# Conditioning products of a two-block transformer: four of six groups summed per partition on VectorE, then one matmul per slice

## The chip, the cores and the metric

The kernel runs on one core of one Trainium2 chip. The metric is the device time of one execution in microseconds, the median of several. In the rows PE is TensorE's matmul, PEld its weight load, DVE is VectorE, ACT is ScalarE, POOL is GpSimd, SP is SyncE, whose queue issues all DMAs here.

## What is computed

Two transformer blocks follow one another on 256 tokens of 1024 features, all in float32. The first has two layers (a stick-breaking and a dilated attention, each with a feed-forward part `ffn1` of width 4096 and a gated per-layer input). The second has two layers (a latent attention with pooling, a grouped attention, each with a convolutional feed-forward part `ffn2`) and a second stream of 256 context tokens. The second block is conditioned: for each of its layers two vectors, the one of the batch (`c`) and the one of the context (`c_ctx`), are multiplied with a matrix of 1024 x 6144. This is the part that the change is about:

```python
    for i in range(DEPTH):
        ...
        ml = (jax.nn.silu(c) @ w_mod[i] + b_mod[i]).reshape(B, N_MOD, 1, D)
        mc = (jax.nn.silu(c_ctx) @ w_mod[i] + b_mod[i]).reshape(N_MOD, D)
        hl = modulate(xl, ml[:, 0], ml[:, 1])
        hc = modulate(xc, mc[0], mc[1])
```

The six rows of 1024 (shift, scale and gate, twice) are taken in three groups of 2048 columns. Of the last layer's second and third group only the row of `c` is used, since the context stream ends there.

## The kernel before

Weights come in tiles of 128 x 1024 float32 through four buffers `ws`; ScalarE rounds each tile to a high part `wh`, VectorE subtracts it to get the low part `wl` (lines 182 and 183, in halves of 512 columns, four buffers each), and TensorE multiplies the three products of high and low parts (lines 194 to 196). The program is written in one order, with generators as fillers: while the main stream goes on, `fill` takes steps from queues, `ctx` (the context stream, which works in the PSUM banks `fx`), `mod` (the conditioning products) and `main`. The numbers of the table `FILL` say how many units of filler go in at each place. Tile's scheduler then sets the order of each engine.

`gemv_gen` computes a group of conditioning rows: for each of eight blocks of 128 input features it loads two `ws` tiles and multiplies them on TensorE, with the two conditioning columns (padded to 32) as weights and four column strips of the array, in one bank `fx` that stays taken until the group is done (line 465). VectorE adds the bias and the one (line 469). Groups 0 and 1 of the first conditioned layer are done in the stick-breaking mixer; group 2 in the first `ffn1`; the second layer's group 0, 1 and 2 in the dilated mixer (where `attend` is the attention of a pair of heads and `proj` projects the next) and in the second `ffn1`. In `ffn1` each of 16 steps is an `up` of the next 256 hidden features, a filler, and a `down` of the last ones.

## Time and profile before

| | |
|---|---|
| median of 3 runs | 1740.43 us (1735.95 to 1746.13) |
| span of the profiled execution | 1732.4 us |
| busy: TensorE / its weight loads | 1662.8 / 1428.1 us |
| busy: VectorE / ScalarE / GpSimd | 1106.5 / 925.7 / 42.3 us |
| DMA | 337.72 MB, 195 GB/s on the mean |
| conditioning matmuls (L465) | 384 records, 65.0 us busy, 35 to 823 us from the start |

The span is that of one execution that the profiler took, from its first to its last instruction; its own device time is not listed, and the span lies 8.0 us below the median of the runs and 3.5 below the lowest. The stretches used below are 190 to 460 us (the first layer's end of mixer, `ffn1` and gate), 460 to 690 (the dilated mixer) and 690 to 900 (the second `ffn1`). Busy times of an engine are a union of its records; matmuls overlap each other in the pipeline, so that the distance between starts says more than the duration of one.

### The profile page before, as it was taken

What the parts mean: (1) busy time and instruction counts of PE and PEld (TensorE: products, weight loads), DVE (VectorE), ACT (ScalarE), POOL (GpSimd) and SP (SyncE); (2) the same over time, 40 slices, a digit from 0 to 9 for tenths busy, and PEclk for the clock granted to TensorE, in tenths of its full rate; (3) what the DMA queues carried; (4) which work ended last, traced back from release to release, by engine and by line L of the source; (5) the groups of instructions that cost most, each with busy time, mean ns of one, the idle gap of its engine ahead of it and who ended that gap; (6) DMA issues with size and microseconds to landing.
All of it is one profiled execution on the core that took longest, in us unless ns stands there. A gap on an engine that the chain in (4) does not pass through costs nothing.

```text
span 1732.4 us, 28608 instructions
## 1 busy us (share of the span) xinstructions
PE 1662.8 (96%) x10465; PEld 1428.1 (82%) x10468; DVE 1106.5 (64%) x2153; ACT 925.7 (53%) x1853; POOL 42.3 (2%) x65
## 2 busy tenths in 40 slices
PE   7998999999999999999999999999999999989997
PEld 6767888987887667888888988988999987779997
DVE  4437644557775446744667777767666887766665
ACT  5536544556654435544556556755555555545554
POOL 0000000000000000000000000000000000000000
PEclk9999999999999999999999999999999999989999
DMA  7777577654666666676756655446666765246663
GB/s 237 259 260 250 178 243 260 215 182 142 212 193 211 206 193 206 198 255 231 226 173 191 201 164 166 131 146 202 188 204 188 244 197 169 67 153 186 186 187 99
DMA packets 301073, 337.72 MB, mean 195 GB/s; under 512 B 18400, under 2 KB 246180, under 8 KB 300932
## 3 DMA queue, kind: packets, MB, share of 16 engines
q1 hardware_dynamic: 300932, 335.89, 61.7%
q8 instruction: 82, 1.34, 0.3%
q14 instruction: 59, 0.48, 0.1%
HBM read 332.57 MB, written 3.24 MB: 194 GB/s over the span
## 4 chain that ended last, share of the span: by engine, by line
PE 45%; DMA 5%; DVE 5%; ACT 2%; issue 1%; POOL 1%; SPq 0%; POOLq 0%; ACTq 0%; DVEq 0%
PE mm L196 6%; PE mm L194 6%; PE mm L195 6%; PE acc L195 5%; PE acc L196 5%; PE acc L194 5%; PE fx L196 3%; PE fx L194 3%; PE fx L195 3%; DMA ws<-in_w_ff_out 2%; DMA ws<-in_w_ff_in 2%; DVE wl L183 2%; PE acc L1007 1%; ACT wh L182 1%; PE mm L1033 1%
## 5 line engine op out<-in xcount | busy, mean ns | idle before, releaser
L183 DVE TENSOR_TENSOR wl<-ws,wh 128x512 fp32r<-128x512 f32 x1004 | 638.9, 668 | 402.7 <-ACT wh L182 391.4
L182 ACT CAST wh<-ws 128x512 fp32r<-128x512 f32 x1004 | 567.4, 603 | 510.3 <-PE mm L195 125.2
L194 PE MATMUL mm<-uh,wh 128*128 128x256 f32 x1344 | 382.8, 285 | 2.9 <-ACT wh L182 2.2
L196 PE MATMUL mm<-uh,wl 128*128 128x256 f32 x1344 | 382.0, 284 | 0.9 <-DVE wl L183 0.9
L195 PE MATMUL mm<-ul,wh 128*128 128x256 f32 x1344 | 381.6, 284 | 0.0
L194 PEld LDWEIGHTS mm<-uh,wh 128*128 128x128 f32 x1344 | 258.7, 192 | 8.7 <-ACT wh L182 3.0
L195 PEld LDWEIGHTS mm<-ul,wh 128*128 128x128 f32 x1344 | 258.8, 193 | 3.0 <-issue 0.4
L196 PEld LDWEIGHTS mm<-uh,wl 128*128 128x128 f32 x1344 | 258.7, 192 | 2.1 <-DVE wl L183 1.9
L194 PE MATMUL acc<-wh,hh 128*128 128x512 f32 x432 | 172.1, 398 | 0.0
L196 PE MATMUL acc<-wh,hl 128*128 128x512 f32 x432 | 169.6, 393 | 0.0
L195 PE MATMUL acc<-wl,hh 128*128 128x512 f32 x432 | 169.2, 392 | 0.0
L194 PEld LDWEIGHTS acc<-wh,hh 128*128 128x128 f32 x432 | 81.3, 188 | 28.7 <-ACT wh L182 5.9
L196 PE MATMUL fx<-uch,wl 128*128 128x256 f32 x352 | 100.6, 286 | 2.9 <-DVE wl L183 2.8
L194 PE MATMUL fx<-uch,wh 128*128 128x256 f32 x352 | 101.0, 287 | 1.7 <-DVE fsum L1191 1.7
L195 PE MATMUL fx<-ucl,wh 128*128 128x256 f32 x352 | 100.4, 285 | 0.0
L196 PEld LDWEIGHTS acc<-wh,hl 128*128 128x128 f32 x432 | 81.2, 188 | 18.3 <-issue 0.8
L195 PEld LDWEIGHTS acc<-wl,hh 128*128 128x128 f32 x432 | 81.4, 188 | 14.8 <-issue 0.4
L194 PE MATMUL mm<-wh,uh 128*128 128x384 f32 (+1 forms) x256 | 86.0, 337 | 2.1 <-ACT wh L182 1.6
L195 PE MATMUL mm<-wl,uh 128*128 128x384 f32 (+1 forms) x256 | 83.3, 325 | 0.6 <-DVE wl L183 0.6
L196 PE MATMUL mm<-wh,ul 128*128 128x384 f32 (+1 forms) x256 | 82.9, 324 | 0.0
L216 POOL TENSOR_TENSOR s<-s,neghalf 128x1 f32<-128x1 f32 (+2 forms) x52 | 38.7, 744 | 1556.5 <-DVE s L214 1556.5
L465 PE MATMUL fx<-ws,cst 128*32 128x512 f32 x384 | 65.0, 607 | 6.7 <-DMA ws<-in_w_mod 5.7
(397 smaller groups left out, 2658.9 us busy)
## 6 DMA issues: line engine op xcount, KB each, us to landing
ws<-in_ffn_w_up SPq DMA_DIRECT2D x528, 128.0 KB
ws<-in_w_mod SPq DMA_DIRECT2D x96, 512.0 KB
ws<-in_ffn_w_down SPq DMA_DIRECT2D x66, 512.0 KB
ws<-in_w_ff_in SPq DMA_DIRECT2D x64, 512.0 KB
ws<-in_w_ff_out SPq DMA_DIRECT2D x64, 512.0 KB
ws<-in_w_in_dil SPq DMA_DIRECT2D x96, 192.0 KB
ws<-in_w_in_sb SPq DMA_DIRECT2D x24, 512.0 KB
row<-mod SPq DMA_DIRECT2D x19, 512.0 KB
```

Source lines behind the costliest of these rows:

```text
L182: act.copy(out=h[:, s], in_=st[:, s])
L183: vec.tensor_sub(out=l[:, s], in0=st[:, s], in1=f32(h[:, s]))
L194: pe.matmul(o, lh, rh, start=start, stop=False)
L195: pe.matmul(o, lh, rl, start=False, stop=False)
L196: pe.matmul(o, ll, rh, start=False, stop=stop)
L216: gp.tensor_tensor(out=r, in0=v, in1=neghalf.to_broadcast([128, w]), op=ALU.pow)
L465: pe.matmul(ps[32 * q:32 * q + 32, :], cst[:, kc, :], st[:, q2 * 512:(q2 + 1) * 512], start=kc == 0, stop=kc == 7)
L1007: pe.matmul(sc[qt][:, n * 256:(n + 1) * 256], q(hd, qt), k(hd, n), start=True, stop=True)
L1033: pe.matmul(o, v(hd, n, kt), PTs[hd][:, 2 * n + kt, :], start=n == 0 and kt == 0, stop=n == nk - 1 and kt == 1)
```

## The change

Four of the six groups leave TensorE's loop. `gemv_vec` loads the same `ws` tiles, but VectorE multiplies a tile with a conditioning value per partition and adds it into an accumulator `ga` of 128 x 1024, over the eight blocks; then four matmuls with `sel` (zero but for its first column, which is one) sum a slice over the partitions. For the groups of which only the row of `c` is used (`nr` = 1) one slice covers all 2048 columns and each tile is read once for one row; with both rows (`nr` = 2) a group has two slices of 1024 columns, and each tile is used for two rows. Group 2 of the first conditioned layer goes into the first `ffn1` (one tile per step), group 0 of the second into the dilated mixer (one tile per `yield` of `attend`), its groups 1 and 2 into the second `ffn1` (two tiles per step). The `mod` queue is empty after the first mixer; so in the last round of the dilated attention `ctx_ok` is true and the context stream fills it. The context fill of the first `ffn1` has 1.6 units in each of 13 steps where it had 5.04 in the four steps after the conditioning group.

```diff
-FILL = dict(sb1=5.0, sb2=1.25, sb3=0.5, sb_end=6.0, sbd=6.0, sbm=0.8, m0=1.0, mix0=8.5, mix1=8.5, f1c=5.04,
+FILL = dict(sb1=5.0, sb2=1.25, sb3=0.5, sb_end=6.0, sbd=6.0, sbm=0.8, m0=1.0, mix0=8.5, mix1=8.5, f1c=1.6,
...
+    sel = const.tile([128, 32], F32, name="sel")
...
+    gp.memset(sel, 0.0)
+    gp.memset(sel[:, 0:1], 1.0)
...
+    def gemv_vec(p, tag, bufs, i, grp, nr):
...
+        w = a["w_mod_2"][i]
+        for half in range(nr):
+            c0 = grp * 2048 + half * 1024
+            accs = [p.tile([128, 2, 512], F32, tag=tag, name="ga", bufs=bufs) for _ in range(2)]
+            for kc in range(8):
+                for hf in range(3 - nr):
+                    st = stage()
+                    c1 = c0 + hf * 1024
+                    nc.sync.dma_start(out=st, in_=w[kc * 128:(kc + 1) * 128, c1:c1 + 1024])
+                    for r in range(nr):
+                        o = accs[hf + r].rearrange("p q n -> p (q n)")
+                        c = cst[:, kc, r:r + 1]
+                        if kc == 0:
+                            vec.tensor_scalar(out=o, in0=st, scalar1=c, scalar2=None, op0=ALU.mult)
+                        else:
+                            vec.scalar_tensor_tensor(out=o, in0=st, scalar=c, in1=o, op0=ALU.mult, op1=ALU.add)
+                    yield
+            clean("ctx")
+            one = one_t[:, grp:grp + 1] if nr == 1 else float(2 * grp + half in (1, 4))
+            bt = fillp.tile([128, 512], F32, tag="xd", name="gvb", bufs=2)
+            gp.memset(bt, 0.0)
+            ps = fx1()
+            mt = tmp((128, 512))
...
+            for q in range(4):
+                pe.matmul(ps[32 * q:32 * q + 32, :], sel, accs[q // 2][:, q % 2, :], start=True, stop=True)
+            vec.scalar_tensor_tensor(out=mt, in0=ps, scalar=one, in1=bt, op0=ALU.add, op1=ALU.add)
...
+            def gemvs():
+                for args in (((0, 2, 2),) if i == 0 else ((1, 1, 1), (1, 2, 1))):
+                    yield from gemv_vec(p, "ga", 2, *args)
+
+            gv = gemvs()
             up(0)
             for g in range(G):
                 if g + 1 < G:
                     up(g + 1)
-                if i == 1 or g_mod0b in queues["mod"]:
-                    fill(1, "mod")
+                next(gv, None)
+                if i == 1:
+                    pass
                 elif g < G - 3:
                     fill(FILL["f1c"])
                 elif g == G - 3:
                     until_dense(FILL["f1d"])
                 if g == G - 2:
+                    clean("ctx")
+                    for _ in gv:
+                        pass
                     before_end()
                 down(g)
+                if i == 1:
+                    next(gv, None)
...
+            gv = gemv_vec(fillp, "c4", 11, 1, 0, 2)
             for qr in range(4):
                 if qr < 3:
                     queues["main"].append(proj(qr + 1))
                 ctx_ok[0] = qr == 3 and not queues["mod"]
                 for t in attend(qr, fx1 if qr < 3 else mm1):
                     work(t)
-                    if qr < 3:
-                        fill(FILL["dlm"], "mod")
+                    next(gv, None)
                 drain_main()
+                if qr == 2:
+                    for _ in gv:
+                        pass
...
-    g_mod0a, g_mod0b, g_mod1 = gemv_gen(0, (0, 1)), gemv_gen(0, (2,)), gemv_gen(1, range(3))
-    queues["mod"].extend([g_mod0a, g_mod0b, g_mod1])
+    g_mod0a = gemv_gen(0, (0, 1))
+    queues["mod"].append(g_mod0a)
```

The scheduler decides where these instructions stand. SP's queue in the second `ffn1`, before (`in_w_ff_in` feeds an `up`, `in_w_ff_out` a `down`, `in_w_mod_2` the conditioning; all go into `ws`, and the numbers are those of single buffers):

```order
L176 DMA ws_7658<-in_w_ff_in 128x4x256
L176 DMA ws_7666<-in_w_ff_in 128x4x256
L462 DMA ws_7730<-in_w_mod_2 128x1024
L462 DMA ws_7734<-in_w_mod_2 128x1024
L176 DMA ws_7738<-in_w_ff_out 128x1024
L176 DMA ws_7758<-in_w_ff_out 128x1024
```

The same queue there after the change:

```order
L490 DMA ws_8129<-in_w_mod_2 128x1024
L177 DMA ws_8132<-in_w_ff_in 128x4x256
L177 DMA ws_8140<-in_w_ff_in 128x4x256
L490 DMA ws_8204<-in_w_mod_2 128x1024
L177 DMA ws_8207<-in_w_ff_out 128x1024
L177 DMA ws_8227<-in_w_ff_out 128x1024
L490 DMA ws_8247<-in_w_mod_2 128x1024
```

The two conditioning loads of a step now stand apart, one behind the `up` loads and one behind the `down` loads, in every step but the last ones.

VectorE in the second `ffn1`, before (`wl` is a half of a weight tile's low part, `r` and `hl` belong to the hidden features):

```order
L623 TENSOR_TENSOR r_7843<-r_7843 128x512
L183 TENSOR_TENSOR wl_7901<-ws_7898,wh_7900 128x512 x2
L200 TENSOR_TENSOR hl_7847<-r_7843,hh_7846 128x512
L183 TENSOR_TENSOR wl_7909<-ws_7906,wh_7908 128x512 x2
L183 TENSOR_TENSOR wl_7981<-ws_7978,wh_7980 128x512 x2
L183 TENSOR_TENSOR wl_8001<-ws_7998,wh_8000 128x512 x2
L623 TENSOR_TENSOR r_7963<-r_7963 128x512
```

And after the change, about the same step:

```order
L201 TENSOR_TENSOR hl_7965<-r_7961,hh_7964 128x512
L184 TENSOR_TENSOR wl_8092<-ws_8089,wh_8091 128x512 x2
L497 SCALAR_TENSOR_TENSOR ga_7613<-ws_8129,cst_102,ga_7613 128x1024
L184 TENSOR_TENSOR wl_8112<-ws_8109,wh_8111 128x512 x2
L497 SCALAR_TENSOR_TENSOR ga_7612<-ws_8204,cst_102,ga_7612 128x1024
L184 TENSOR_TENSOR wl_8135<-ws_8132,wh_8134 128x512 x2
L184 TENSOR_TENSOR wl_8143<-ws_8140,wh_8142 128x512
L665 TENSOR_TENSOR r_8079<-r_8079 128x512
```

The six halves between `hl` and the next `r` follow each other before; now a multiply-add `ga` stands behind the first pair and another behind the second, five and three rows ahead of the next `r`.

VectorE in the dilated mixer at the first softmax of the third pair of heads, before (`s` and `P` are the softmax's sums and probabilities, `acc` its scores):

```order
L683 TENSOR_REDUCE s_6363<-acc_6353 128x1
L685 TENSOR_SCALAR s_6365<-s_6363 128x1
L183 TENSOR_TENSOR wl_6482<-ws_6478,wh_6481 128x512
L183 TENSOR_TENSOR wl_6482<-ws_6478,wh_6481 128x256
L689 RECIPROCAL s_6369<-s_6367 128x1
L683 TENSOR_REDUCE s_6373<-acc_6353 128x1
L690 TENSOR_SCALAR P_6362<-P_6362,s_6369 128x384
```

And after the change at the same place:

```order
L736 TENSOR_REDUCE s_6348<-acc_6338 128x1
L497 SCALAR_TENSOR_TENSOR ga_6268<-ws_6564,cst_102,ga_6268 128x1024
L738 TENSOR_SCALAR s_6350<-s_6348 128x1
L497 SCALAR_TENSOR_TENSOR ga_6269<-ws_6564,cst_102,ga_6269 128x1024
L742 RECIPROCAL s_6354<-s_6352 128x1
L736 TENSOR_REDUCE s_6358<-acc_6338 128x1
L743 TENSOR_SCALAR P_6347<-P_6347,s_6354 128x384
```

Two multiply-adds now stand inside the softmax, between the maximum (L736) and the normalisation (L743), where a tile's two `wl` stood; both read the same `ws` tile.

## Rows read from the trace of the kernel before

**Rows 1.** The page, part 1: busy us of each engine, share of the span, instructions.

```profile
PE 1662.8 (96%) x10465; PEld 1428.1 (82%) x10468; DVE 1106.5 (64%) x2153; ACT 925.7 (53%) x1853; POOL 42.3 (2%) x65
```

**Rows 2.** The page, part 4: shares by engine of the chain that ended last.

```profile
PE 45%; DMA 5%; DVE 5%; ACT 2%; issue 1%; POOL 1%; SPq 0%; POOLq 0%; ACTq 0%; DVEq 0%
```

**Rows 3.** Timeline of TensorE, second `ffn1`, with a filler: start us, us, instruction.

```profile
746.24 1.07 PE L465 MATMUL fx<-ws,cst 128*32 128x512 f32 x8
...
747.23 0.50 PE L194 MATMUL acc<-wh,hh 128*128 128x512 f32 x1
...
759.66 0.50 PE L194 MATMUL acc<-wh,hh 128*128 128x512 f32 x1
```

**Rows 4.** The same timeline, later steps without a filler.

```profile
847.69 0.40 PE L194 MATMUL acc<-wh,hh 128*128 128x512 f32 x1
...
858.91 0.40 PE L194 MATMUL acc<-wh,hh 128*128 128x512 f32 x1
```

**Rows 5.** Stretches: busy us (records) of PE, PEld, DVE, ACT, POOL; clock, DMA share, GB/s.

```profile
460.00:690.00 230.00, 219.75 (x1258) 168.80 (x1261) 128.18 (x314) 110.63 (x251) 4.57 (x7) 0.99 0.65 201
690.00:900.00 210.00, 205.61 (x1333) 179.85 (x1332) 122.47 (x197) 104.30 (x190) 2.57 (x4) 1.00 0.67 219
610.00:620.00 10.00, 6.92 (x41) 5.44 (x38) 4.92 (x14) 4.22 (x12) 0.00 (x0) 0.91 0.73 225
620.00:630.00 10.00, 10.00 (x44) 6.63 (x43) 4.04 (x12) 3.83 (x10) 0.00 (x0) 0.75 0.26 79
760.00:780.00 20.00, 20.00 (x124) 17.11 (x123) 10.22 (x17) 8.44 (x15) 0.00 (x0) 1.00 0.84 283
```

**Rows 6.** The same view, line L465 (conditioning matmuls) alone.

```profile
190.00:460.00 270.00, 8.52 (x64) 1.26 (x64) 1.00 0.63 207
460.00:690.00 230.00, 26.22 (x128) 3.60 (x128) 0.99 0.65 201
690.00:900.00 210.00, 8.53 (x64) 1.26 (x64) 1.00 0.67 219
```

**Rows 7.** Waits of TensorE's weight loads, 460 to 690: us, times, longest.

```profile
PEld fx L465 <- DMA ws<-in_w_mod: 7.2, 6, 3.5
...
PEld fx L760 <- DVE wl L183: 1.2, 2, 0.8
...
PEld fx L760 <- DVE s L685: 0.8, 1, 0.8
```

**Rows 8.** Groups of VectorE by shape, whole span: busy us, mean ns, idle before.

```profile
L183 DVE TENSOR_TENSOR wl<-ws,wh 128x512 fp32r<-128x512 f32 x934 | 613.8, 687 | 397.0 <-ACT wh L182 385.7 <-issue 0.3
...
L481 DVE SCALAR_TENSOR_TENSOR h<-t,s,h 128x1024 f32<-128x1024 f32 x8 | 10.2, 1278 | 0.0
...
L690 DVE TENSOR_SCALAR P<-P,s 128x768 f32<-128x768 f32 x8 | 4.9, 613 | 0.0
...
L469 DVE SCALAR_TENSOR_TENSOR t<-fx,misc,gvb 128x512 f32<-128x512 f32 x6 | 4.5, 749 | 8.0 <-PE fx L465 8.0
```

**Rows 9.** Timelines of SP's queue, ScalarE and TensorE, second `ffn1`.

```profile
744.00 1.62 SPq L176 DMA_DIRECT2D ws<-in_w_ff_in  x2
...
747.33 0.81 SPq L462 DMA_DIRECT2D ws<-in_w_mod  x2
...
748.91 0.62 ACT L182 CAST wh<-ws 128x512 fp32r<-128x512 f32 x1 [4.50 <-DMA ws<-in_w_ff_in]
...
758.66 1.06 PE L465 MATMUL fx<-ws,cst 128*32 128x512 f32 x8
```

**Rows 10.** ScalarE's casts, 720 to 820: busy us, mean ns, idle before by releaser.

```profile
L182 ACT CAST wh<-ws 128x512 fp32r<-128x512 f32 x60 | 34.5, 618 | 53.8 <-DMA ws<-in_w_ff_in 27.2 <-DMA ws<-in_w_ff_out 25.9 <-PE mm L195 0.3
```

**Rows 11.** Timeline of TensorE, second layer's `ffn2`, steps without a filler.

```profile
1606.25 0.40 PE L194 MATMUL acc<-wh,hh 128*128 128x512 f32 x1
...
1614.75 0.40 PE L194 MATMUL acc<-wh,hh 128*128 128x512 f32 x1
```

**Rows 12.** Line L465, whole span: what TensorE idled for before it, us, times.

```profile
  DMA ws<-in_w_mod: 16.0, 16
```

More of the change, by code (lines that the diff above doesn't have):

```diff
@@ L474, in gemv_gen @@
             yield 0.1
+    def gemv_vec(p, tag, bufs, i, grp, nr):
[23 more added lines that the diff above has]
+            for q in range(4):
+                c1 = c0 + (q if nr == 1 else q % 2) * 512
+                nc.sync.dma_start(out=bt[32 * q:32 * q + 1, :], in_=a["b_mod_2"][i:i + 1, c1:c1 + 512])
+            for q in range(4):
+                pe.matmul(ps[32 * q:32 * q + 32, :], sel, accs[q // 2][:, q % 2, :], start=True, stop=True)
+            vec.scalar_tensor_tensor(out=mt, in0=ps, scalar=one, in1=bt, op0=ALU.add, op1=ALU.add)
+            for q in range(4):
+                c1 = c0 + (q if nr == 1 else q % 2) * 512
+                r = 0 if nr == 1 else q // 2
+                nc.sync.dma_start(out=mod[i][r:r + 1, c1:c1 + 512], in_=mt[32 * q:32 * q + 1, :])
+            yield
+        mod_done.add((i, grp))
     def post_norm(y, g, tt):
@@ L1108, in ffn2 @@
                     up(f + 1)
-                if i == 0 and g_mod1 in queues["mod"]:
-                    fill(1, "mod")
-                elif i == 0 and f < NCH - 3:
+                if i == 0 and f < NCH - 3:
                     credit["ctx"] += FILL["f2c"]
```

## The prediction

> **What bounds the kernel now.** I read the busy times first: TensorE is busy for 96% of the span, VectorE 64%, ScalarE 53% [rows 1], and the chain that ended last is mostly TensorE's [rows 2]. A busy matmul engine may still be one that waits inside its pipeline, so the next view is the distance between starts. In the second layer's `ffn1` one loop step (an `up`, a filler, a `down`) takes 759.66 - 747.23 = 12.43 us while the filler is a conditioning step [rows 3], and 858.91 - 847.69 = 11.22 us once there is no filler [rows 4]. Steps that repeat like this while VectorE is busy only 122 of that stretch's 210 us [rows 5] are steps of a full TensorE. So a conditioning step (8 matmul records) costs 12.43 - 11.22 = 1.21 us of the end time there, somewhat more than the 1.07 us that its records show [rows 3].
>
> Where the removed work sits comes from its line cut into stretches: 64 records in the first layer's `ffn1` (190 to 460), 128 in the dilated mixer (460 to 690), 64 in the second `ffn1` (690 to 900) [rows 6]. That is 8, 16 and 8 steps; the other 128 of 384 lie earlier and stay. The dilated mixer is less clean: 128 records there are busy 26.22 us, 1.64 us a step, and TensorE's weight loads wait 7.2 us for these very transfers [rows 6, 7].
>
> **The change part by part.**
>
> *Removed.* 32 steps of 1.21 us: -9.68 us in each `ffn1`, -19.36 us in the mixer.
>
> *Added on TensorE.* Six slices end with four matmuls (8 records) of the form of the old ones, so 1.21 us each, two in each stretch: +2.42 us three times. That leaves -7.26, -16.94 and -7.26 us, together -31.5 us.
>
> By the busy rows alone it would be -43.27 + 43.27 x 48/256 = -35.2 us [rows 6]. The Trainium skill ("Trainium Kernel Development and Optimization", Performance Expectations) calls matmul busy time a bad metric because matmuls are pipelined. By that rule the sum from starts, -31.5 us, is the one to keep; the trace agrees, since 1.64 us of busy per step in the mixer stands against 1.21 us between starts.
>
> *Added on VectorE.* 84 multiply-adds of 128x1024 with two tensors and a column: the same operation and shape takes 1278 ns at L481 [rows 8], 107 us together. 12 products of 128x1024 with a column: nearest row 613 ns for 768 elements [rows 8], scaled 0.82 us, 10 us. VectorE goes from 1106 to about 1223 us, 72% of the new span. Locally, a step of the second `ffn1` has ten operations of about 0.687 us (eight `wl`, `r`, `hl`) [rows 8] and now two of 1.28: 9.4 us in 11.22. It fits, and the cover is the 1.8 us left. Were that gone (VectorE at 11.5 us), each step would lose 0.3 us. A multiply-add would have to take (11.22 - 6.87)/2 = 2.2 us before VectorE became the limit; I take 1.28, since shape, operation and memory are those of the row.
>
> *The new wait.* At the end of a slice VectorE waits for the four matmuls, as it does today at L469 [rows 8]: 8.0 us over six, thus 1.3 us each, and this now happens eight times instead of six. Behind it stand the `wl` of the next weights. Two more such waits, 2.7 us, are below what the range holds; I take nothing.
>
> *Feed.* The second `ffn1` now has two conditioning loads in all but the last steps, as the filled steps have today, but a step shall last 11.22 us instead of 12.43: six loads of 524 KB, 280 GB/s instead of 253. It has run at 283 GB/s over 20 us in that very stretch [rows 5]. The four `ws` buffers must turn over in 4/6 of a step, 7.5 us. A weight load issued at 744.00 is taken up by ScalarE at 748.91, 4.9 us later [rows 9]; two casts and two subtractions and the issue bring that to about 7.3 us, a conditioning load to about 6.6. Today the conditioning loads sit longer: issued at 747.33, used by TensorE at 758.66, over 11 us [rows 9]. So it fits narrowly, and ScalarE already waits for loads much of the time [rows 10]. Bounds: 0, or the pace of today (12.43 us in all 16 steps, which is +17 us against the sum). I take +2 us, near the lower end, because of the 283 GB/s.
>
> *Mixer.* Here the removed steps were also cover for the softmax chain on VectorE and ScalarE, while multiply-adds now stand in that chain's queue. On the other side the 7.2 us of waits for the loads can vanish. Bounds: -7.2 us, or one 1.28 us multiply-add ahead of each of the 15 chain steps of three head pairs, +19.2 us, plus a fall of the clock like the one at 610 to 630, where TensorE was busy 6.92 of 10 us and the granted clock then stood at 0.91 and 0.75, part of the time at 1.2 instead of 2.4 GHz (0.9 + 2.5 = 3.4 us lost) [rows 5]: +22.6 us. Today that chain is late by under 1 us at a time [rows 7]. I take 0: the two cancel.
>
> *Moved.* The context fill of the first `ffn1` is spread as 13 x 1.6 = 20.8 units where it was 4 x 5.04 = 20.2: nothing. With `mod` empty, the last attention round of the mixer is filled with context work that came later before, down to the first `ffn2`. That stage stays full without it: in the second layer, with no filler, steps repeat at 1614.75 - 1606.25 = 8.50 us and so does the next [rows 11]. Nothing; if that cover failed, some of the 18.8 units that the round asks for (3.38 + 7.65 + 2 x 2.4 + 3.0, about a us each) would be missed later. 16 more short bias loads and stores (0.3 to 0.4 us each on SP as other issues [rows 9]) hide in SP's idle time; 6 us if not. The two extra memsets lie on GpSimd, idle all but 42 us [rows 1].
>
> **Sum:** -31.5 + 2.0 = -29.5 us. The profiled execution has a span of 1732.4 us, 8.0 below the median of the runs, 1740.43; keeping that distance, 1702.9 of span and **1711 us** measured (-1.7%). This case's own range is 1704 to 1719: the two extra waits, the feed between 0 and twice what I took, and a mixer that keeps or loses 5 us.
>
> **Rivals.**
>
> *More than the sum.* All 7.2 us of waits for the loads vanish and the feed costs nothing: -31.5 - 7.2 = -38.7, 1702 us. For it: conditioning loads no longer wait 11 us for TensorE's turn. Against: the chain in the mixer loses cover.
>
> *The loads pace the second `ffn1`.* 16 steps at 12.43 us are 198.9 us against 8 x 12.43 + 8 x 11.22 = 189.2 today: +9.7 there instead of -5.3, in all -14.5, 1726 us. For it: ScalarE's waits [rows 10]; against: 283 GB/s.
>
> *The mixer gives it back* (the change frees TensorE only for it to idle): -7.3 - 5.3 + 5.7 = -6.9, 1734 us, no measurable change. For it: the chain's rows from VectorE are there already [rows 7]; against: VectorE is busy 128 of 230 us there, and 39 us more still leave a quarter.
>
> *Slower, by VectorE's queue.* Each of the 64 loads is now awaited on VectorE, and the `wl` of the next weights stand behind. TensorE's waits for such loads were 16.0 us in 16 times [rows 12]; at 1.0 us for every load, all passed on, +64 - 31.5 = +32.5, 1773 us. It cancels the gain at 0.49 us a load and makes the kernel slower beyond the measurement's reach at 0.63. The Trainium skill ("TensorE: Matmul & The Clock Gate", Architectural detail) says that VectorE is strict FIFO; no run here shows it yet. By that rule nothing can pass a waiting multiply-add. Against the rival: the loads are issued in the order in which VectorE takes them, and there are four buffers.
>
> **Chances.** Forecast 0.50, more 0.15, loads pace 0.13, mixer gives back 0.14, slower 0.08. A difference under 0.5% (8.7 us) can hardly be told from none here. Forecast, more and loads pace lie beyond it on the fast side: faster 0.78. The mixer case and a little of its neighbours: same 0.14; slower 0.08. The range runs from a little under the second case to the mixer case, 1698 to 1735; it leaves out the slower case and the tail of the mixer's.
>
> **What would show it.** Right: steps of about 11.2 to 11.4 us in both `ffn1`, 48 matmul records at the new line, multiply-adds of about 1.28 us, VectorE near 1223 us, TensorE's busy time lower by about 35 us, no waits of TensorE for conditioning loads after 200 us. Wrong: steps of 12 us or more in the second `ffn1` with ScalarE or VectorE waiting for loads (feed), idle TensorE before L813 and L833's transposes in the mixer with a granted clock under 0.97 there (chain), or `wl` late behind a multiply-add that waits for its load (queue).

## The result and the profile after

The changed kernel takes 1723.22 us (median of 4 runs, 1721.61 to 1724.47) against 1742.59 for the kernel before (4 runs, 1735.95 to 1746.13): a ratio of 0.9892, 95% interval 0.9866 to 0.9919. It is faster, by 19.4 us or 1.1%, beyond the 0.5% that can be told from nothing. The forecast was 1711 us with 1704 to 1719 as its own range, so the sign and the wide range (1698 to 1735) held, and the size did not: the time lies 12 us above the forecast, and of the 29.5 us that were to be gained 10 are missing.

The traced execution has a span of 1720.3 us, 12.1 less than that of before. Since one run here took 1722.1 us with a span of 1720.3, the span of 1732.4 before belongs, by the same distance, to an execution of some 1734 us (an estimate), at the low end of its kernel's; the last 7 us of the difference between the medians lie in executions of which there is no trace.

First the page's line on engines, which answers to [rows 1]:

```profile
PE 1635.5 (95%) x10259; PEld 1428.7 (83%) x10260; DVE 1211.1 (70%) x2251; ACT 926.6 (54%) x1854; POOL 44.6 (3%) x69
```

TensorE's busy time fell by 27.3 us (about 35 were expected) and VectorE's rose by 104.6 (117 were expected). The prices of the new instructions were near, as the groups of VectorE by shape show (columns as in [rows 8]):

```profile
L497 DVE SCALAR_TENSOR_TENSOR ga<-ws,cst,ga 128x1024 f32<-128x1024 f32 x84 | 106.3, 1281 | 57.7 <-DMA ws<-in_w_mod 57.5
L495 DVE TENSOR_SCALAR ga<-ws,cst 128x1024 f32<-128x1024 f32 x12 | 8.7, 749 | 1.9 <-DMA ws<-in_w_mod 1.9
```

A multiply-add takes 1.281 us where 1.278 was taken, a product 0.749 where 0.82 was. What was not in the sum stands behind the second bar, the idle time ahead of these instructions: VectorE waited 57.5 + 1.9 us for these 64 loads, 0.93 us each.

Where the time went is read by stages. Each `ffn1` is counted from the first matmul of its first `up` to the start of the last `acc<-wh,hh` of its last `down`, read from TensorE's timeline; the mixer from the gate's products behind the first `ffn1` to the second `ffn1`. The borders of the mixer and of the second `ffn1`, before and then after:

```profile
452.13 0.39 PE L194 MATMUL acc<-wh,uh 128*128 128x512 f32 x1
...
705.72 0.39 PE L194 MATMUL mm<-uh,wh 128*128 128x256 f32 x1 [0.33 <-DVE ul L200]
...
903.44 0.39 PE L194 MATMUL acc<-wh,hh 128*128 128x512 f32 x1
```

```profile
452.60 0.39 PE L195 MATMUL acc<-wh,uh 128*128 128x512 f32 x1
...
696.99 0.39 PE L195 MATMUL mm<-uh,wh 128*128 128x256 f32 x1
...
903.53 0.39 PE L195 MATMUL acc<-wh,hh 128*128 128x512 f32 x1
```

| stage | before | after | change | forecast |
|---|---|---|---|---|
| up to the first `ffn1` | 203.3 | 205.3 | +2.0 | 0 |
| first `ffn1` | 228.9 | 227.7 | -1.2 | -7.3 |
| up to the gate's products | 19.9 | 19.6 | -0.3 | 0 |
| gate's products and dilated mixer | 253.6 | 244.4 | -9.2 | -16.9 |
| second `ffn1` | 197.7 | 206.5 | +8.8 | -5.3 |
| up to the next gate's products | 17.0 | 20.7 | +3.7 | 0 |
| latent attention and first `ffn2` | 487.8 | 470.2 | -17.6 | 0 |
| the rest | 324.2 | 325.9 | +1.7 | 0 |

The mixer, the gate behind the second `ffn1` and the first `ffn2` belong together: 17.8 us of context products (106 more matmul records, start to start) moved into the mixer's last round, 3.7 us (39 records) into that gate, and they are missing later. By subtraction the mixer without them became 27 us shorter. The busy times, clock and DMA of the mixer and the second `ffn1`, the first two stretches of [rows 5]:

```profile
460.00:690.00 230.00, 221.30 (x1332) 191.25 (x1332) 182.35 (x381) 127.73 (x285) 6.21 (x10) 0.99 0.63 188
690.00:900.00 210.00, 194.72 (x1199) 170.99 (x1198) 149.54 (x216) 93.82 (x170) 1.48 (x2) 0.98 0.77 249
```

In the mixer VectorE is busy 182 of 230 us. The granted clock is 0.99 as before, and the loads that TensorE waited for in [rows 7] are no longer among its waits. In the second `ffn1` TensorE is busy 10.9 us less, and the stage nevertheless takes longer. Its step, from TensorE's timeline as in [rows 3]:

```profile
758.87 0.40 PE L195 MATMUL acc<-wh,hh 128*128 128x512 f32 x1
...
772.35 0.40 PE L195 MATMUL acc<-wh,hh 128*128 128x512 f32 x1
...
785.85 0.40 PE L195 MATMUL acc<-wh,hh 128*128 128x512 f32 x1
```

13.48 and 13.50 us, where 11.22 was expected and 12.43 stood before. Not all steps are like these: of the 13 distances from the first `down` to the 14th, six are 11.22 to 11.47 us and seven 12.5 to 14.0 (two of these at the end of the first group). In the long ones TensorE waits for a low part that VectorE makes late (between 710 and 830 us; us in total, times, longest), which it did for 0.2 us before:

```profile
PE mm L197 <- DVE wl L184: 7.1, 5, 2.0
```

The timelines of SP's queue, ScalarE and VectorE in the step from 758.87 on say why:

```profile
757.07 0.38 SPq L177 DMA_DIRECT2D ws<-in_w_ff_in  x1
759.60 0.34 SPq L490 DMA_DIRECT2D ws<-in_w_mod  x1
...
761.73 0.62 ACT L183 CAST wh<-ws 128x512 fp32r<-128x512 f32 x1 [0.32 <-DMA ws<-in_w_ff_in]
762.26 0.59 ACT L664 ACTIVATE r<-mm 128x512 f32<-128x512 f32 x1
...
764.54 1.28 DVE L497 SCALAR_TENSOR_TENSOR ga<-ws,cst,ga 128x1024 f32<-128x1024 f32 x1 [3.77 <-DMA ws<-in_w_mod]
765.74 1.89 DVE L184 TENSOR_TENSOR wl<-ws,wh 128x512 fp32r<-128x512 f32 x3
767.55 0.69 DVE L665 TENSOR_TENSOR r<-r 128x512 f32<-128x512 f32 x1
768.15 0.68 DVE L184 TENSOR_TENSOR wl<-ws,wh 128x512 fp32r<-128x512 f32 x1
...
771.57 1.29 DVE L497 SCALAR_TENSOR_TENSOR ga<-ws,cst,ga 128x1024 f32<-128x1024 f32 x1 [0.76 <-DMA ws<-in_w_mod]
...
778.04 1.28 DVE L497 SCALAR_TENSOR_TENSOR ga<-ws,cst,ga 128x1024 f32<-128x1024 f32 x1 [3.98 <-DMA ws<-in_w_mod]
```

The conditioning load is issued at 759.60, and VectorE stands idle for 3.77 us until it can be read. Behind it stand the low parts of two tiles that ScalarE cast from 760.27 on, and the square of `r`, which ScalarE had made by 762.85. The second `up` tile was issued at 757.07 and is let go at 768.83: its buffer was held for 11.8 us, where the working said 7.3. SP then waits for buffers, and the next loads come late. The Trainium skill ("TensorE: Matmul & The Clock Gate", Architectural detail) calls VectorE's queue strict FIFO; the trace agrees here: `r` stood ready for 4.7 us, and in the first 1.7 of them the engine did nothing.

From the multiply-add at 764.54 to the one at 778.04 are 13.50 us: 8.7 of work on VectorE and 0.76 + 3.98 of waits for two loads, with nothing else between. So in this stretch the step is as long as VectorE's work and waits together. Later steps with the same work are 11.22 us because the waits are short. VectorE's waits for the loads over three long steps (745 to 786 us) and over three short ones (826 to 859):

```profile
DVE ga L497 <- DMA ws<-in_w_mod: 16.1, 7, 4.0
```

```profile
DVE ga L497 <- DMA ws<-in_w_mod: 3.0, 4, 1.0
```

Why the later loads come in time is not shown by any run.

### The profile page after: what moved, and what is told of

The parts are those of the page before. It is cut to its first block, busy times and chain, and to the rows that moved or that the text cites. A ratio compares the mean times of both kernels' runs of the same rounds, so it can differ in the third digit from the quotient of the medians.

```text
span 1720.3 us, 28310 instructions
## 1 busy us (share of the span) xinstructions
PE 1635.5 (95%) x10259; PEld 1428.7 (83%) x10260; DVE 1211.1 (70%) x2251; ACT 926.6 (54%) x1854; POOL 44.6 (3%) x69
## 4 chain that ended last, share of the span: by engine, by line
PE 55%; DVE 14%; DMA 13%; issue 4%; ACT 3%; SPq 1%; POOL 1%; ACTq 0%; POOLq 0%; DVEq 0%
PE mm L195 6%; PE mm L196 6%; PE mm L197 6%; PE acc L197 6%; PE acc L196 6%; PE acc L195 6%; DMA ws<-in_w_mod 6%; DVE wl L184 5%; PE fx L195 4%; PE fx L196 4%; PE fx L197 4%; DMA ws<-in_w_ff_in 2%; DVE ga L497 2%; DMA ws<-in_w_in_dil 2%; ACT wh L183 1%
## 5 line engine op out<-in xcount | busy, mean ns | idle before, releaser
L184 DVE TENSOR_TENSOR wl<-ws,wh 128x512 fp32r<-128x512 f32 (+1 forms) x1004 | 638.1, 668 | 273.3 <-ACT wh L183 261.5
L183 ACT CAST wh<-ws 128x512 fp32r<-128x512 f32 (+1 forms) x1004 | 568.6, 604 | 477.8 <-PE mm L196 132.7
L497 DVE SCALAR_TENSOR_TENSOR ga<-ws,cst,ga 128x1024 f32<-128x1024 f32 x84 | 106.3, 1281 | 57.7 <-DMA ws<-in_w_mod 57.5
L195 PEld LDWEIGHTS acc<-wh,hh 128*128 128x128 f32 x432 | 82.2, 190 | 17.6 <-issue 1.6
```

Source lines behind the costliest of these rows:

```text
L183: act.copy(out=h[:, s], in_=st[:, s])
L184: vec.tensor_sub(out=l[:, s], in0=st[:, s], in1=f32(h[:, s]))
L195: pe.matmul(o, lh, rh, start=start, stop=False)
L497: vec.scalar_tensor_tensor(out=o, in0=st, scalar=c, in1=o, op0=ALU.mult, op1=ALU.add)
```

## The experiments

**The second `ffn1`: whose fault is it?** Three edits, each alone in the changed kernel, and one that spreads the load. Each ratio is to the kernel before as measured beside the run; the changed kernel was not measured again, so differences to it of a few us whose ratios overlap its own (0.9866 to 0.9919) are no firmer than that. First, its two groups back on TensorE:

```diff
-            gv = gemvs()
+            gv = gemvs() if i == 0 else iter(())
+            g_ff = gemv_gen(1, (1, 2)) if i == 1 else None
+            if i == 1:
+                queues["mod"].append(g_ff)
...
                 if i == 1:
-                    pass
+                    fill(1, "mod")
```

> Only the two groups of the second ffn1 go back to TensorE's loop; the other two stay on VectorE. That stage takes 206.5 us after the change (697.0 to 903.5 in the trace) and took 197.7 before (705.7 to 903.4). Theory 1 (loads that are awaited on VectorE, and a burst of them at the end, cost more than the removed matmuls gave): the stage returns to about 198 us, the span falls by about 9 us to 1711, measured 1713 against 1723. Theory 2 (the 8.8 us are a shift between stages, work that was late anyway): the span stays at 1718 to 1722.

Measured 1737.39 us (7 runs, 1728.05 to 1743.34; ratio to before 0.9963, 0.9937 to 0.999), 14 us slower than the changed kernel. The stage took 212.8 us and the gate behind it 6 us more. Neither theory's number: my comparison with before was wrong, since before held 8 conditioning steps in this stage and this kernel 16 (the other 8 were in the mixer). With equal work, VectorE is much the cheaper place even with its waits.

Second, the loads left out:

```diff
-                    st = stage()
-                    c1 = c0 + hf * 1024
-                    nc.sync.dma_start(out=st, in_=w[kc * 128:(kc + 1) * 128, c1:c1 + 1024])
+                    if get:
+                        st = get()
+                    else:
+                        st = stage()
...
+            get = (lambda: h[:, 0, :]) if i == 1 else None
```

> In the second ffn1 the multiply-adds read a tile that lies in SBUF all the time (the residual), and the 32 conditioning loads are left out, so two conditioning rows are wrong. All VectorE work stays. Theory 1 (the wait for loads): steps of 11.2 to 11.5 us all through, the stage about 190 us (197.7 - 8 x 1.21 + 2.4), span about 1704. Rival (VectorE's own time for the multiply-adds is the cost): steps stay at 13 to 14 us while they run, stage over 203 us, span over 1717.

Measured 1710.30 us (one run), span 1708.5; the steps 11.22 us but for two at the end of the first group (13.97 and 12.42), the stage 185.8. With no load to stand behind, the scheduler put up to five multiply-adds into one step and none into others, and those with five are 11.22 us too. Full multiply-adds cost nothing when they wait for nothing: the rival (VectorE's own time) falls, in the form that its time by itself is the cost. Third, the loads kept and the multiply-adds made short:

```diff
-                        if kc == 0:
+                        if nr == 1 and kc:
+                            o = o[:, 0:16]
+                            vec.scalar_tensor_tensor(out=o, in0=st[:, 0:16], scalar=c, in1=o, op0=ALU.mult, op1=ALU.add)
+                        elif kc == 0:
```

> In the second ffn1 all conditioning loads stay and are awaited on VectorE at the same places, but 28 of 32 multiply-adds work on 16 columns of 1024 (their sums are wrong). Theory 1 (the wait at the head of VectorE's queue and the four buffers): most of the loss stays, steps of 12.3 to 13.5 us, the stage 200 to 206 us, span 1714 to 1720. Rival (VectorE's own time): steps of 11.2 us, the stage about 191, span 1705.

Measured 1712.69 us (one run), span 1710.9, the stage 196.3; steps of 11.22 us with all loads in place (11.69 to 13.97 around the end of the first group), though VectorE still waited for them between 720 and 830 us, longer than in the changed kernel (there first, then here):

```profile
DVE ga L497 <- DMA ws<-in_w_mod: 25.3, 12, 4.0
```

```profile
DVE ga L496 <- DMA ws<-in_w_mod: 29.9, 13, 4.7
```

My theory 1 falls too, in the form that the wait by itself is the cost. What remained was the end of the stage. The two runs bracket the cost: 8.7 us of VectorE's work and more fit into 11.22 us, and so do 6.6 of work with 4 to 5 of waiting; 8.7 with 4.7 do not, and the step grows to their sum. Why the loads are late is then a third theory, a loop. Each of six tiles holds one of four buffers from its issue until VectorE has read it; waits and operations on VectorE lengthen the holding, and late buffers make late loads.

The end of the stage has a cause of its own. In the changed kernel the generator is emptied at the last step but one. SP's queue, ScalarE, and the stretches of the stage's end there:

```profile
871.36 9.16 SPq L490 DMA_DIRECT2D ws<-in_w_mod  x5
```

```profile
886.89 1.14 ACT L183 CAST wh<-ws 128x512 fp32r<-128x512 f32 x2 [7.28 <-DMA ws<-in_w_ff_out]
```

```profile
880.00:892.00 12.00, 8.04 (x49) 5.66 (x48) 9.59 (x13) 4.45 (x9) 0.00 (x0) 0.88 0.87 295
892.00:904.00 12.00, 12.00 (x46) 9.65 (x46) 7.25 (x13) 5.78 (x12) 0.55 (x1) 0.83 0.63 191
```

Five conditioning loads pass ahead of the last weights, ScalarE waits 7.28 us for these, TensorE is busy 8.04 of 12 us, and the granted clock stands at 0.88 and then 0.83, part of the time at 1.2 instead of 2.4 GHz. From the 14th `down` on it takes 32.6 us to the stage's last `acc<-wh,hh`, against 22.1 before and 23.0 in the run without the loads. The 14th `down` before and then after:

```profile
881.35 0.40 PE L194 MATMUL acc<-wh,hh 128*128 128x512 f32 x1
```

```profile
870.93 0.40 PE L195 MATMUL acc<-wh,hh 128*128 128x512 f32 x1
```

The edit against it:

```diff
                 if i == 1:
                     next(gv, None)
+                    if g in (1, 3, 5, 7):
+                        next(gv, None)
```

> As the changed kernel, but in four of the early steps of the second ffn1 a third conditioning tile is taken, so that none is left over for the end, where now five loads in a row stand ahead of the last weights (the last two steps and the end take 32.6 us from the 14th down on, 22.1 before). Theory 1a (the burst by itself costs about 10 us, and an earlier tile costs about 2 us in its step, four of them): the stage falls by 2 to 10 us, span 1711 to 1718, and ScalarE's wait of 7.3 us before the last weights is gone. Rival (the loads cost the same wherever they stand): span 1720 to 1724.

Measured 1720.20 us (4 runs, 1717.23 to 1726.36; ratio to before 0.9856, 0.9831 to 0.988), 3 us under the changed kernel with overlapping runs. The stage took 203.9 us in the trace, which is of the slowest of the four runs: the end is shorter (28.1 us from the 14th `down` on), but three steps near those in which a third tile was taken became 15.0 to 16.6 us.

**Testing the loop.** One extra buffer for every other conditioning tile; the places in the program stay, and two masks share their memory to make room (`dm0 = sbm`):

```diff
+            def get():
+                turn.append(0)
+                if i == 1 and len(turn) % 2:
+                    return p.tile([128, 1024], F32, tag="wg", name="wg", bufs=1)
+                return stage()
...
-                    st = stage()
+                    st = get() if get else stage()
```

> As the changed kernel, but in the second ffn1 every other conditioning tile goes into one extra buffer instead of one of the four ws (places in the program, loads and multiply-adds unchanged; two masks share their memory to make room). Theory 3 (a loop: four buffers must turn over for six tiles, and each is held while its reader waits in VectorE's queue): steps of 11.2 to 11.8 us for most of the stage, which takes 190 to 198 us instead of 206.5; measured 1708 to 1716. Rival (VectorE's time and the loads' bandwidth add up whatever the buffers): the stage stays at 203 to 208, measured 1720 to 1726.

Measured 1710.28 us (4 runs, 1709.30 to 1717.39; ratio to before 0.9832, 0.9794 to 0.9869): 13 us under the changed kernel. The stage took 190.7 us. Four of its steps, from TensorE's timeline:

```profile
737.05 0.40 PE L195 MATMUL acc<-wh,hh 128*128 128x512 f32 x1
...
781.93 0.40 PE L195 MATMUL acc<-wh,hh 128*128 128x512 f32 x1
```

44.88 us, 11.22 each. These four are no clean test, though: with a buffer of its own the scheduler takes some tiles earlier (six are issued ahead of the first `down`, where it was three), and three of the four hold one multiply-add instead of two. ScalarE's waits between 720 and 830 us (us in total, times, longest), in the changed kernel and then with the fifth buffer:

```profile
ACT wh L183 <- DMA ws<-in_w_ff_in: 27.3, 15, 3.6
ACT hh L200 <- DVE r L665: 23.5, 8, 4.9
```

```profile
ACT wh L183 <- PE mm L196: 22.9, 13, 3.1
...
ACT hh L200 <- DVE r L665: 9.0, 9, 3.6
ACT wh L183 <- DMA ws<-in_w_ff_in: 6.8, 4, 2.8
```

ScalarE now waits for TensorE to free a high part, so TensorE bounds these steps again. (The 27.3 us of waits for loads are not by themselves the sign of long steps: the run with the short multiply-adds has 28.2 of them.) A part of the gain, the shorter end above all, may come from the order. Cleaner is the comparison of the last two runs below, one program but for the fifth buffer. With the buffer the first six steps are 11.22 us each, the second and third of them with three multiply-adds (721.77 to 744.21):

```profile
721.77 0.40 PE L195 MATMUL acc<-wh,hh 128*128 128x512 f32 x1
...
744.21 0.40 PE L195 MATMUL acc<-wh,hh 128*128 128x512 f32 x1
```

Without it the first six are 11.22, 11.22, 11.39, 13.79, 12.78 and 15.27 us (14 multiply-adds in all, with it 11), and the stage takes 199.1 us instead of 185.8. So the fifth buffer does what the theory says; how much of it is turnover and how much order is not shown. A control on the kernel before:

```diff
+            if i == 1:
+                extra[0] = lambda: p.tile([128, 1024], F32, tag="wg", name="wg", bufs=1)
...
-                    st = stage()
+                    st = extra[0]() if extra[0] and hf else stage()
```

> A control: the kernel before, with every other conditioning tile of its second ffn1 (8 of 16) in one extra buffer; all products stay on TensorE. Theory 3 says that the change itself turned that stage from one that TensorE bounds into one that the four buffers bound: then the extra buffer gives nothing here, steps stay at 12.43 us with a filler, the stage at 196 to 199 us (197.7 before), the time within 1738 to 1746. Rival (one more buffer helps that stage with either kernel): the stage shorter by 5 us or more, measured 1737 or less.

Measured 1740.39 us (10 runs, 1735.48 to 1746.31; ratio 0.999, 0.9968 to 1.0011): no difference. Steps with a filler stayed at 12.43 us; the stage took 194.4, a little under the band. By this control a shortage of buffers is the change's own.

A more thorough version of the same idea went wrong, and tells something too: two own buffers, loads one tile ahead, one accumulator at a time.

```diff
...
+            while plan and len(held) < 2:
+                kc, c1 = plan.pop(0)
+                st = p.tile([128, 1024], F32, tag="wg", name="wg", bufs=2)
+                nc.sync.dma_start(out=st, in_=w[kc * 128:(kc + 1) * 128, c1:c1 + 1024])
+                held.append(st)
+            return held.pop(0)
...
```

> In the second ffn1 the conditioning tiles get two buffers of their own and are loaded one tile ahead of their multiply-add; one accumulator is summed after the other (to make room), and four early steps take a third tile, so that none is left for the end. Loads and multiply-adds are all there. Both leaving out the loads and shortening the multiply-adds had brought the steps to 11.2 us, so theory 3 is a loop: a buffer comes free only after the wait in VectorE's queue, and the four must turn over for six tiles. By it the steps are 11.2 to 11.8 us, the stage (697.0 to 903.5, 206.5 us) takes 190 to 196, measured 1709 to 1714. Rival (loads and multiply-adds just add up, bandwidth or VectorE time): steps of 12.5 us or more, the stage over 202, measured over 1718.

Measured 1759.68 us (4 runs, 1752.83 to 1762.20; ratio to before 1.0106, 1.0068 to 1.0144): slower than both kernels. The steps were 11.22 us and the stage 184.7, but the scheduler took only 10 of the 32 tiles ahead of the loop's last weights and put the rest behind. TensorE's timeline after the stage:

```profile
901.32 1.92 PE L553 MATMUL fx<-ga,sel 128*32 128x512 f32 x4 [5.38 <-DVE ga L549]
925.54 1.92 PE L553 MATMUL fx<-ga,sel 128*32 128x512 f32 x4 [22.30 <-DVE ga L549]
```

TensorE stood idle for 5.38 and 22.30 us for sums that used to be done by then; the gate behind the stage took 69.5 us instead of 20.7. This run neither supports nor speaks against the loop, since steps with so few tiles would be quick by either theory.

**The first `ffn1`: the context stream.** Its gain was forecast at 7.3 us and came out at 1.2. TensorE's idle times of over 1 us there, from its timeline:

```profile
244.18 0.31 PE L965 MATMUL fx<-ident,qtok 128*96 128x128 f32 x1 [1.18 <-ACT qtok L977]
...
285.21 0.39 PE L195 MATMUL fx<-ck,wh 128*128 128x256 f32 x1 [1.98 <-ACT qT L968]
...
367.31 2.07 PE L1035 MATMUL fx<-t,ws 128*128 128x256 f32 x4 [2.35 <-ACT t L1032]
...
396.42 0.44 PE L1074 MATMUL fx<-ident,P 128*128 128x128 f32 x2 [1.16 <-DVE PT L1078]
```

6.7 us, all of it ahead of context matmuls (`fx`) that wait for a small operation of the same stream. Before, TensorE was idle 0.9 us in that stage in gaps of over 0.3 us. The edit puts the context work where it was:

```diff
-... mix1=8.5, f1c=1.6,
+... mix1=8.5, f1c=5.04,
...
+                elif g < 9:
+                    pass
                 elif g < G - 3:
                     fill(FILL["f1c"])
```

> As the changed kernel, but the context stream fills the first ffn1 as before: nothing in the first nine steps, then 5.04 units in each of four. That stage took 228.9 us before (203.3 to 432.2), 227.7 after (205.3 to 433.0), where 7.3 us less were forecast. Theory A (spread thinly over 13 steps, the context stream's chains of small operations stand open and TensorE idles in front of their matmuls, some 7 us in four stretches): the stage falls to 221 to 224 us, measured 1716 to 1720. Theory B (the multiply-adds and their loads on VectorE make the weights' low parts late): the stage stays at 226 to 229 us, measured 1721 to 1726.

Measured 1717.80 us (4 runs, 1713.86 to 1718.62; ratio to before 0.9864, 0.9826 to 0.9901), 5.4 us under the changed kernel. The stage took 222.7 us; in the nine traces that spread the context work it took 226.9 to 233.2, in the two later ones with this edit 223.1 and 226.5. But the gate behind it took 22.8 us instead of 19.6, since ten context records and the last sum's eight matmul records now stand there: for both stages together 245.4 against 247.3. And theory B is not out. The first three steps are 11.22 us with a conditioning tile in each, so there the products on VectorE are free; the next four, which have no context work either, are 11.35 to 13.16. VectorE and TensorE in the longest of these:

```profile
266.25 2.48 DVE L497 SCALAR_TENSOR_TENSOR ga<-ws,cst,ga 128x1024 f32<-128x1024 f32 x2 [3.36 <-DMA ws<-in_w_mod]
268.65 1.28 DVE L184 TENSOR_TENSOR wl<-ws,wh 128x512 fp32r<-128x512 f32 x2
```

```profile
269.38 0.39 PE L197 MATMUL mm<-uh,wl 128*128 128x256 f32 x1 [1.32 <-DVE wl L184]
```

A low part stands behind a multiply-add that waits for its load, as in the second `ffn1`, and TensorE idles for it. So both theories hold in part; the traces give the context stream's chains 1.9 us over the two stages, the medians 5.4.

**The mixer.** The context work taken out of its last round:

```diff
-                ctx_ok[0] = qr == 3 and not queues["mod"]
+                ctx_ok[0] = False
```

> As the changed kernel, but the last round of the dilated attention takes no context work (as before). The forecast took this move at nothing. If so: the mixer (452.6 to 697.0 us, 244.4 us) becomes 16 to 20 us shorter, the first ffn2 (1187 to 1395) as much longer, and the time stays within 1720 to 1726. Rival (without that cover TensorE idles in the last round, which is what the change gained there): the mixer shortens by less than 10 us and the time rises to 1729 or more.

Measured 1727.96 us (10 runs, 1717.99 to 1737.50; ratio to before 0.9931, 0.9901 to 0.996). The mixer became 14.7 us shorter (229.7 us, 23.9 less than before), the gate behind the second `ffn1` 3.7 shorter, and the first `ffn2` (its first `up` to its last `down`) 11.0 longer, 218.0 us as before; with the latent attention ahead of it 20.6 longer. The move is worth between nothing and some 5 us; the runs overlap with those of the changed kernel, and neither expectation was met.

And its group of products back on TensorE:

```diff
-            gv = gemv_vec(fillp, "c4", 11, 1, 0, 2)
+            g_mx = gemv_gen(1, (0,))
+            queues["mod"].append(g_mx)
...
-                    next(gv, None)
+                    if qr < 3:
+                        fill(FILL["dlm"], "mod")
...
-                    for _ in gv:
-                        pass
+                    drain(g_mx, "mod")
```

> As the changed kernel, but group 0 of the second layer, in the dilated mixer, goes back to TensorE's loop (8 steps of 8 matmuls). Theory 1 (each such step costs 1.2 us of matmul and up to 0.9 us in which TensorE waits for its load; 16 matmuls at the slices' ends go): the mixer lengthens from 244 to 253 to 258 us, measured 1731 to 1737. Rival (the step price of the clean ffn1 loop, 1.21 us, without waits: 9.7 - 2.4): the mixer at 250 to 253, measured 1728 to 1731. If the mixer's gain came from the context work instead: no change, 1720 to 1726.

Measured 1732.97 us (10 runs, 1728.72 to 1739.07; ratio to before 0.9958, 0.9938 to 0.9977), the mixer 257.1 us, as theory 1 has it: 12.7 us more for 8 conditioning steps in place of the two sums, 1.6 us a step on balance where the working had 0.91 (7.26 over 8). In time it is 9.8 us; the changed mixer's stage takes 241.9 to 251.0 us in the ten traces that have it, so the 12.7 could be 6 to 15. Its gain came from the products.

**Together.** The edit for the context stream with the spread end, and then with the fifth buffer too:

> The two edits that each measured lower than the changed kernel, together: the context stream in the first ffn1 as before (1717.8 alone) and the second ffn1's conditioning tiles spread so that none is left for the end (1720.2 alone). If the two stages are independent, as their traces say: 1723.2 - 5.4 - 3.0 = 1715, within 1711 to 1719. Rival (what is gained in one is lost in the other or between): 1718 or more.

> The fifth buffer, the context stream as before and the spread tail together. If theory 3 holds: 1723.2 - 5.4 - 10 = about 1707, within 1702 to 1713. If the fifth buffer gives nothing: as the run with the other two edits, 1711 to 1719.

Measured 1713.82 us (4 runs, 1711.74 to 1721.34; ratio to before 0.9855, 0.9809 to 0.9901) and 1703.07 us (4 runs, 1701.91 to 1709.86; ratio 0.979, 0.9752 to 0.9827). Both lie in their bands, and the last is 20 us under the changed kernel and 2.1% under the kernel before. Its second `ffn1` took 185.8 us.

## Why the prediction was right and wrong

**Right.** The removed work was where the rows said, 48 matmul records remained at the new line, the multiply-adds on VectorE cost what was taken, and VectorE's total did not bound the kernel. The mixer's chain did not suffer: the rival in which it gives the gain back did not come.

**The step that failed: the feed of the second `ffn1`.** "So it fits narrowly" was worked out from buffers that turn over in 7.3 us, durations of a pipeline in which VectorE takes a tile when it is cast. After the change a tile also stands behind a multiply-add that waits for another load, and one was held for 11.8 us. The term was +2 us and measured +16.1 (8.8 against the -7.3 without it), near the upper bound of +17 that the working had set aside. Against the run without the loads the stage lost 20.7 us, 11.1 between the first and the 14th `down` and 9.6 behind it; without loss it would have been 4.6 us shorter than the sum had it (185.8 against 197.7 - 7.26). Both of the prediction's own signs for this came, the feed's and the queue's. The rival "the loads pace the second `ffn1`" had +9.7 for the stage, against +8.8 measured. That it came so near is in part luck: its 16 steps of 12.43 us did not come, but seven long steps, others of 11.22 us and a long end. The 283 GB/s of [rows 5] said that the transfers can run that fast, which they did without the stage needing it: 249 GB/s over the stretch. The cover that the working named, 1.8 us of free VectorE per step, counted its work and not its waits, and was no cover against 4 to 5 us of waiting at the head of the queue in a step. The Trainium skill ("Perfetto Trace Analysis", Optimization Strategy) says that a gap that repeats on the engine that should be saturated can mean too few buffers for the next tile; the run with the fifth buffer agrees, with 13.5 us steps that became 11.22, in part with fewer tiles in them.

The rival "slower, by VectorE's queue" had its condition met almost exactly (1.0 us for each of 64 loads assumed, 0.93 measured) and its price not: most of the 59 us were not passed on, since a wait costs only what VectorE's free time in the step doesn't cover. In the run with the short multiply-adds 29.9 us of such waits left the steps at 11.22 us.

**The last steps of that stage** were named ("in all but the last steps") and not costed. Five loads in a row ahead of the last weights cost about 10 us there, with the granted clock at 0.88 and 0.83.

**The first `ffn1`** was to gain 7.3 us and gained 1.2. "Nothing" for the context fill was wrong by 2 us in the traces of that stage and its gate, and by up to 5 in the medians: the same units in smaller portions leave the chains between them open. The rest is not resolved; the late low parts shown above, in four steps that together are 4 us over 11.22, point at VectorE's queue here too, for which the working had no term in this stage.

**The mixer** was mis-sized the other way. The sum took -16.94 and let the waits for the loads cancel against the chain; without the moved context work it measured -27 by subtraction and -23.9 in the run that leaves the move out. 112 conditioning records fewer alone took 23.7 us less from start to start (25.7 to 2.0), about the sum's -16.94 with the 7.2 us of [rows 7] on top, -24.1: the rival "more than the sum", in this stage. The price of 1.21 us came from the second `ffn1`; in the mixer the 128 records took 25.7 us, 1.61 a step. A whole step takes 1.0 us from its first record to the next other matmul in either stage, but some steps of the mixer stand in pieces and take 1.65 us and more. The prediction's comparison of 1.64 us busy with 1.21 between starts was therefore one of two stages, and the trace does not bear out its choice of -31.5 over the -35.2 from busy times.

**The moved context work** was taken at nothing: 17.8 us into the mixer, 3.7 into the gate behind the second `ffn1` (16.9 us in the run without the move, 17.0 before, 20.7 after), 17.6 out of the stages behind. That is a loss of 4 us in this pair of traces; against the trace without the move it is a gain of 2 (14.7 and 3.7 in, 20.6 out), and the medians of that run leave up to 5 open. "Nothing" is right to within these.

With these the sum reads -1.2 - 27.0 + 17.8 + 3.7 + 8.8 - 17.6 and 3.4 us of small differences (+2.0, -0.3, +1.7), -12 in the pair of traces. Open stays what the kernel before does in its executions of up to 1746 us: its one trace, and that of the control (span 1735.5; 229.0, 253.3 and 194.4 us for the first `ffn1`, the mixer and the second `ffn1`), are from the low end.

## What to carry to other kernels

When work moves to an engine that takes its instructions in order, a free share of its time is not enough: each operand that it may have to wait for holds up all that stands behind. Add the waits to the work before comparing with the step. Count buffers by holding time, from a load's issue to its last reader, against buffers times the step, and count it with the new waits in it. And cost the ends of a loop and the size of a filler's portions as carefully as the steady state; here the end was worth 10 us beside a gain of 19, the portions 2 to 5.

## What was not expected of the hardware

A price from one row of the same operation and shape was good to 0.3% (1.278 and 1.281 us), while a holding time put together from such rows was off by 60%. TensorE idling for a third of 12 us at the end of the second `ffn1` was followed by a granted clock of 0.83 in the next 12 us, in which it was busy throughout. And the changed kernel's executions lie within 3 us of each other, where those of the kernel before spread over 10 (four runs of each); no run here says why.
